# Weight parts and activations at the same offset modulo 256 bytes in a two-layer trunk

## The chip, the cores and the metric

The kernel runs on one core of a Trainium2 chip. The metric is the device time of one execution in microseconds (us); lower is better. TensorE (PE) multiplies, VectorE (DVE) and ScalarE (ACT) work elementwise, GpSimd (POOL) does a few small operations, and the DMA engines bring weights from HBM into SBUF, the on-chip memory of 128 partitions.

## What is computed

Two layers of a decoder trunk on 256 tokens of width 1024, in float32. A layer is a half-step FFN, four token mixers beside each other with gated merging, and a second half-step FFN. Almost all of the arithmetic is products of the activations with large weight matrices:

```
for l in range(DEPTH):
    h = _rmsnorm(x, ffn1_norm[l])
    x = x + 0.5 * _swiglu(h, ffn1_w_gate[l], ffn1_w_up[l], ffn1_w_down[l])   # 1024 -> 2816 -> 1024
    h = _rmsnorm(x, mix_norm[l])
    ... = jnp.split(h @ w_in[l], IN_SPLIT_POINTS, axis=-1)                    # 1024 -> 12288
    y_a, y_b, y_c, y_d = _hgrn2(...), _s5(...), _conformer_conv(...), _dilated_attention(...)
    merged = sum over k of gates[:, :, k] * (y_k @ w_branch[l, k])            # 512 -> 1024 each
    x = x + merged @ w_out[l]
    h = _rmsnorm(x, ffn2_norm[l])
    x = x + 0.5 * _swiglu(h, ffn2_w_gate[l], ffn2_w_up[l], ffn2_w_down[l])
return _rmsnorm(x, final_norm)
```

## The kernel before

**Three products for one.** TensorE reads operands of type float32r, of less precision than float32. So each operand is split in two: a high part, the value rounded to that type, and a low part, what is left. A product is then three matmuls into one PSUM bank (high by high, high by low, low by high):

```
def mm3(o, ah, al, bh, bl, first, last):
    T.matmul(o, ah, bh, start=first, stop=False)
    T.matmul(o, ah, bl, start=False, stop=False)
    T.matmul(o, al, bh, start=False, stop=last)
```

The first operand of `T.matmul` after the output is the stationary one (128 columns, loaded ahead of the matmul; the profile shows the load as PEld LDWEIGHTS), the second one streams through (the moving one).

**The weight stream.** `Stream` brings the weights through 512 slots of 1024 elements per partition, in the order in which they are used. A DMA on SyncE's queue lands 1 MB in one of four buffers `raw`; ScalarE writes the high part of a slot into one of six buffers `whi`, VectorE the low part into one of five buffers `wlo`:

```
self.act.activation(hv, src, AF.Copy)
self.dve.tensor_tensor(lv, src, hv.bitcast(F32), op=ALU.subtract)
```

Both run ahead of the matmuls by as many slots as there are buffers. Everything else (norms, evacuations, the mixers' small operations) is put between these by a planner that keeps an estimated clock for each engine; its order is fixed when the program is made.

**Two forms of product.** Activations are held feature-major, as parts `hTh` and `hTl` (after a norm), `gh` and `gl` (inside an FFN), `yAh` and so on (of the mixers).

- `cols_feat` and `rows_feat` make feature-major results: the weight part is stationary, the activations move, 256 columns. These are `gate_h` and `up_h` (FFN chunks 1 to 5), `pu_h`, `pf_h`, `pq_h`, `pb_h`, `pa_h`, `pgt_h` (mixer projections and gates), `glu` and `br`.
- `cols_tok` and `down` make token-major results: the activations are stationary, the weight part moves, 512 columns. These are `gate_t`, `up_t` (FFN chunk 0), `pi_t`, `pg_t`, `att_t`, `po_t` and `down`.

`down` sums over k = 0 to 21 (128 of the 2816 features each) into four banks, two token halves by two halves of the width. For k = 0 to 16 the four go together; for k = 17 to 21 first the one token half and then the other, and there k = 20 and 21 come last, first for the one half of the width and then for the other (6 matmuls each). The last FFN's second token half ends the program's matmuls.

**Where the tiles lie.** A pool gives each tag its buffers when the tag is first asked for, one after the other in a partition, with no alignment beyond 32 bytes. In bytes from the partition's start:

| tag | first buffer | step | start modulo 256 | holds |
|---|---|---|---|---|
| `ident`, `x0`, `x1` | 16512, 17024, 21120 | | 128 | identity, residual |
| `heap` | 25216 | 4096 | 128 | `hTh`, `hTl`, `gh0` to `gh4`, `gl0` to `gl4`, the mixers' parts, gates |
| `raw` | 119424 | 8192 | 128 | landed weights |
| `half` | 152256 | 2048 | 192 | `gh5`, `gl5` (the last chunk of 256), `sg`, `pT`, other temporaries |
| small constants | 172736 to 179391 | | various | `vcol` ... `amask`, `hmask`, `four`, `r4`, `mi`, `diag`, norm scalars |
| `whi` | 179392 | 4096 | 192 | high parts of the weights |
| `wlo` | 203968 | 4096 | 192 | low parts of the weights |
| small scratch | 224448 to 228511 | | various | `ropeA`, `ropeB`, softmax scalars, statistics |

The slices that a matmul takes of a tile begin at multiples of 512 bytes in it, so they keep the tile's offset modulo 256.

Of the kernel before, what the change touches and what calls it, by code (L numbers as in the profile page):

```python
# [19 lines left out]
P = 128  # L20
# [168 lines left out]
def trunk(ctx, tc, x_in, positions, ffn1_norm, ffn1_w_gate, ffn1_w_up, ffn1_w_down, mix_norm, w_in,  # L189
# [11 lines left out]
    def const(shape, name, dtype=F32):  # L201
        return sb.tile(shape, dtype, tag=name, name=name, bufs=1)
# [244 lines left out]
    amask = const([P, 3, 256], "amask")  # L447
    hmask = const([P, 4, 64], "hmask", mybir.dt.uint8)
    four = const([P, P], "four", I32)

    def range_reduce(dst, src, tag):
        k = H2(list(src.shape), "rr_k" + tag)
        V.tensor_scalar(k, src, 1.0 / TWO_PI, None, op0=ALU.mult)
        V.tensor_scalar(k, k, MAGIC, None, op0=ALU.add)
        V.tensor_scalar(k, k, MAGIC, None, op0=ALU.subtract)
        V.scalar_tensor_tensor(dst, k, -CW1, src, op0=ALU.mult, op1=ALU.add)
        V.scalar_tensor_tensor(dst, k, -CW2, dst, op0=ALU.mult, op1=ALU.add)
        V.scalar_tensor_tensor(dst, k, -CW3, dst, op0=ALU.mult, op1=ALU.add)
        V.tensor_scalar(dst, dst, math.pi, -math.pi, op0=ALU.min, op1=ALU.max)
# [1205 lines left out]
```

## Time and profile before

| | |
|---|---|
| three runs | 1583.33, 1577.35, 1583.43 us; median 1583.33 |
| the profiled execution | 1577.96 us, span 1576.3 us, mean granted TensorE clock 0.998 |
| busy in the span | PE 1550.6 us (98%), DVE 1106.4 (70%), ACT 839.6 (53%), POOL 28.1 (2%) |
| read from HBM | 277.53 MB, 178 GB/s over the span |

The span is the time from the first to the last instruction of one profiled execution; the device time beside it has 1.66 us more around it. The rows further down come from that execution. Nearly all instructions stand under L72, the line of the helper that issues them, so the names of the tiles tell them apart: `gate_h<-hTh,wlo` is a matmul into a bank of `gate_h` that reads `hTh` and `wlo`, without buffer numbers. A matmul's listed duration reaches from its start until its results are out, and overlaps with its neighbours'. The distance from one start to the next is what the stream of matmuls costs.

### The profile page before, as it was taken

To read this page: it belongs to the slowest core of one execution; us is meant where nothing else is said; L and a number is where in the kernel's file an instruction comes from. 1 tells how busy PE (TensorE), PEld (TensorE's weight loads), DVE (VectorE), ACT (ScalarE), POOL (GpSimd) and SP (SyncE) were. 2 spreads that over 40 slices of the span, in tenths; PEclk is the share of its full clock that TensorE was granted. 3 is DMA by queue.
4 is the path that set the end of the run, shared out by engine and by line. 5 is a ranking of instruction groups with operands and counts; after the bars stand their busy time and mean duration, and the time that the engine had idled before them with its cause. 6 is when DMAs were issued, how large, how long until landed. Compare 5 with 4: busy or idle time off the path is not lost.

```text
span 1576.3 us, 27619 instructions
## 1 busy us (share of the span) xinstructions
PE 1550.6 (98%) x11407; PEld 1417.4 (90%) x11407; DVE 1106.4 (70%) x1797; ACT 839.6 (53%) x1209; POOL 28.1 (2%) x58
## 2 busy tenths in 40 slices
PE   7999999999999999999999999999999999999998
PEld 5999789889899998999889988987899999989986
DVE  6778865976878866555478874568768897765553
ACT  5545555567565465444445543656665555554442
POOL 2000000000000000000000000000000000000000
PEclk9999999999999999999999999999999999999999
DMA  7565556553544556555565555665345445655551
GB/s 275 198 173 200 194 179 204 161 173 122 161 161 161 170 184 222 188 189 212 174 180 188 188 187 191 206 193 172 116 150 171 160 161 178 211 183 181 188 207 56
DMA packets 179518, 282.46 MB, mean 179 GB/s; under 512 B 26718, under 2 KB 82080, under 8 KB 179392
## 3 DMA queue, kind: packets, MB, share of 16 engines
q1 hardware_dynamic: 154240, 270.55, 51.4%
q10 hardware_dynamic: 24832, 9.97, 2.6%
q8 instruction: 89, 1.46, 0.4%
q14 instruction: 37, 0.30, 0.1%
q0 software_dynamic: 320, 0.18, 0.0%
HBM read 277.53 MB, written 3.15 MB: 178 GB/s over the span
## 4 chain that ended last, share of the span: by engine, by line
PE 91%; DVE 3%; ACT 2%; ACTq 1%; DMA 1%; issue 1%; POOL 0%; SPq 0%; POOLq 0%; DVEq 0%
PE down L72 15%; PE up_h L72 12%; PE gate_h L72 12%; PE att_t L72 11%; PE pgt_h L72 11%; PE br L72 6%; PE po_t L72 3%; PE gate_t L72 3%; PE up_t L72 2%; PE pi_t L72 1%; PE pb_h L72 1%; PE pu_h L72 1%; PE pf_h L72 1%; PE pa_h L72 1%; PE glu L72 1%; PE hl L72 1%
## 5 line engine op out<-in xcount | busy, mean ns | idle before, releaser
L72 DVE TENSOR_TENSOR wlo<-raw,whi 128x1024 fp32r<-128x1024 f32 x512 | 614.8, 1220 | 194.0 <-ACT whi L72 98.8
L72 ACT ACTIVATE whi<-raw 128x1024 fp32r<-128x1024 f32 x512 | 526.2, 1055 | 180.5 <-PE down L72 97.5
L72 PE MATMUL gate_h<-hTh,wlo 128*128 128x256 f32 x576 | 160.2, 278 | 2.8 <-DVE wlo L72 2.8
L72 PE MATMUL gate_h<-hTh,whi 128*128 128x256 f32 x576 | 161.1, 280 | 0.0
L72 PE MATMUL up_h<-hTh,whi 128*128 128x256 f32 x576 | 160.8, 279 | 0.2 <-ACT whi L72 0.2
L72 PE MATMUL up_h<-hTh,wlo 128*128 128x256 f32 x576 | 160.0, 278 | 0.8 <-DVE wlo L72 0.8
L72 PE MATMUL up_h<-hTl,whi 128*128 128x256 f32 x576 | 160.0, 278 | 0.0
L72 PE MATMUL gate_h<-hTl,whi 128*128 128x256 f32 x576 | 159.9, 278 | 0.0
L72 PE MATMUL pgt_h<-hTh,whi 128*128 128x256 f32 x512 | 145.6, 284 | 0.0
L72 PE MATMUL pgt_h<-hTl,whi 128*128 128x256 f32 x512 | 142.6, 279 | 0.0
L72 PE MATMUL pgt_h<-hTh,wlo 128*128 128x256 f32 x512 | 142.6, 279 | 0.0
L72 PE MATMUL down<-whi,gh 128*128 128x512 f32 x352 | 138.8, 394 | 0.0
L72 PE MATMUL down<-whi,gl 128*128 128x512 f32 x352 | 138.6, 394 | 0.0
L72 PE MATMUL down<-wlo,gh 128*128 128x512 f32 x352 | 138.2, 393 | 0.0
L72 PE MATMUL att_t<-whi,hTh 128*128 128x512 f32 x288 | 117.7, 409 | 0.0
L72 PE MATMUL att_t<-whi,hTl 128*128 128x512 f32 x288 | 113.5, 394 | 0.0
L72 PE MATMUL att_t<-wlo,hTh 128*128 128x512 f32 x288 | 113.0, 392 | 0.0
L72 PEld LDWEIGHTS gate_h<-hTh,wlo 128*128 128x128 f32 x576 | 108.2, 188 | 3.4 <-DVE wlo L72 3.4
L72 PEld LDWEIGHTS up_h<-hTh,whi 128*128 128x128 f32 x576 | 108.9, 189 | 0.6 <-ACT whi L72 0.4
L72 PEld LDWEIGHTS up_h<-hTh,wlo 128*128 128x128 f32 x576 | 108.1, 188 | 1.0 <-DVE wlo L72 1.0
L72 PEld LDWEIGHTS gate_h<-hTh,whi 128*128 128x128 f32 x576 | 108.8, 189 | 0.1
L72 PEld LDWEIGHTS gate_h<-hTl,whi 128*128 128x128 f32 x576 | 108.2, 188 | 0.0
(385 smaller groups left out, 3333.1 us busy)
## 6 DMA issues: line engine op xcount, KB each, us to landing
raw<-in_w_in_dram SPq DMA_DIRECT2D x60, 1024.0 KB, 5.1
raw<-in_ffn_w_up_dram SPq DMA_DIRECT2D x44, 1024.0 KB, 5.3
raw<-in_ffn_w_down_dram SPq DMA_DIRECT2D x44, 1024.0 KB, 4.9
raw<-in_ffn_w_gate_dram SPq DMA_DIRECT2D x42, 1024.0 KB, 5.1
raw<-in_w_in_dram SPq DMA_DIRECT2D x72, 512.0 KB, 4.7
raw<-in_w_branch_dram SPq DMA_DIRECT2D x16, 1024.0 KB, 5.1
raw<-in_w_out_dram SPq DMA_DIRECT2D x8, 1024.0 KB, 5.2
raw<-in_s_w_glu_dram SPq DMA_DIRECT2D x16, 256.0 KB, 3.8
```

The source lines that it names most:

```text
L72: return f(*args, **kw)
```

## The change

One tag is added to the pool, right behind `four`: a tile of 48 floats per partition, 192 bytes, that nothing writes or reads.

```
 amask = const([P, 3, 256], "amask")
 hmask = const([P, 4, 64], "hmask", mybir.dt.uint8)
 four = const([P, P], "four", I32)
+const([P, 48], "gap")
```

All tags that are first asked for after it begin 192 bytes further: `r4`, `mi`, `diag`, the norm's scalars, `whi` (179584, that is 128 modulo 256), `wlo` (204160, 128 modulo 256) and the small scratch at the end. `ident`, `x`, `heap`, `raw` and `half` stay where they are. No instruction is added, removed or moved.

## Rows read from the trace of the kernel before

**Rows 1.** Part 1 of the page: busy us, share of the span, instructions
```profile
PE 1550.6 (98%) x11407; PEld 1417.4 (90%) x11407; DVE 1106.4 (70%) x1797; ACT 839.6 (53%) x1209; POOL 28.1 (2%) x58
```

**Rows 2.** Waits of PE, longest first in total: us, times, longest us
```profile
PE xT L72 <- DVE xn L72: 9.1, 1, 9.1
PE hl L72 <- DVE KL L72: 3.3, 2, 1.7
PE gate_h L72 <- DVE wlo L72: 2.8, 2, 2.1
```

**Rows 3.** PE's groups, by form: count | busy us, mean ns of one | idle before
```profile
L72 PE MATMUL gate_h<-hTh,whi 128*128 128x256 f32 x576 | 161.1, 280 | 0.0
...
L72 PE MATMUL pgt_h<-hTh,whi 128*128 128x256 f32 x512 | 145.6, 284 | 0.0
...
L72 PE MATMUL down<-whi,gh 128*128 128x512 f32 x352 | 138.8, 394 | 0.0
...
L72 PE MATMUL att_t<-whi,hTh 128*128 128x512 f32 x288 | 117.7, 409 | 0.0
...
L72 PE MATMUL gate_t<-whi,hTh 128*128 128x512 f32 x64 | 26.7, 418 | 0.6 <-ACT hTh L72 0.6
...
L72 PE MATMUL pu_h<-hTh,whi 128*128 128x256 f32 x64 | 17.8, 279 | 0.0
...
L72 PE MATMUL pi_t<-whi,hTh 128*128 128x512 f32 x32 | 12.8, 400 | 0.0
```

**Rows 4.** The chain in order of time: start us, us, engine, line, count
```profile
222.21 11.31 PE pu_h L72 x96
...
287.05 19.25 PE att_t L72 x84
...
441.69 8.48 PE pgt_h L72 x72
478.55 9.90 PE pgt_h L72 x84
522.33 12.72 PE pgt_h L72 x108
...
572.72 10.88 PE br L72 x96
...
652.99 10.88 PE gate_h L72 x96
...
729.15 58.37 PE down L72 x255
...
1428.65 11.31 PE gate_h L72 x96
...
1507.80 53.20 PE down L72 x228
```

**Rows 5.** Busy us of each engine in two stretches, granted clock, DMA share, GB/s
```profile
652.99:718.27 65.28, 65.28 (x578) 65.28 (x578) 36.47 (x36) 30.16 (x36) 0.00 (x0) 1.00 0.60 197
1417.35:1496.50 79.15, 79.15 (x674) 79.15 (x674) 41.36 (x41) 35.18 (x42) 0.00 (x0) 1.00 0.56 186
```

**Rows 6.** Timeline of PE at the end: start us, us of one matmul
```profile
1562.18 0.39 PE L72 MATMUL down<-whi,gh 128*128 128x512 f32 x1
...
1566.30 0.39 PE L72 MATMUL down<-whi,gh 128*128 128x512 f32 x1
1568.80 0.39 PE L72 MATMUL down<-whi,gl 128*128 128x512 f32 x1
```

**Rows 7.** VectorE's and ScalarE's groups, by form, as in rows 3
```profile
L72 DVE TENSOR_TENSOR wlo<-raw,whi 128x1024 fp32r<-128x1024 f32 x512 | 614.8, 1220 | 194.0 <-ACT whi L72 98.8 <-PE down L72 64.8 <-PE gate_h L72 12.0
L72 ACT ACTIVATE whi<-raw 128x1024 fp32r<-128x1024 f32 x512 | 526.2, 1055 | 180.5 <-PE down L72 97.5 <-PE br L72 19.5 <-issue 13.5
...
L72 DVE TENSOR_TENSOR gl<-sg,gh 128x512 fp32r<-128x512 f32 x36 | 24.9, 693 | 25.1 <-ACT gh L72 25.1
...
L72 DVE TENSOR_TENSOR mrg<-mrg,gate 128x512 f32<-128x512 f32 x24 | 16.6, 692 | 0.8
```

More of the change, by code (lines that the diff above doesn't have):

```diff
@@ L449, in trunk @@
     four = const([P, P], "four", I32)
+    const([P, 48], "gap")
     def range_reduce(dst, src, tag):
```

## The prediction

> **What bounds the kernel now.** I read the page first for the share of the engines: TensorE is busy 98% of the 1576.3 us span, VectorE 70%, ScalarE 53% [rows 1]. The list of TensorE's own waits comes next, longest first: 9.1 us in one wait at the start, then 3.3 and 2.8 us [rows 2]. So the end is set by how fast TensorE goes from one matmul to the next; nobody keeps it waiting. The profiled run took 1577.96 us, 1.66 more than its span. The median of the runs is 1583.33, and two of the three lie there; the third, 1577.35, lies by the profiled one. I work from 1577.96 and come back to the gap of 5.4 below.
>
> **How fast the matmuls follow each other.** The busy time of a matmul overlaps its neighbour's, so the groups [rows 3] are of use for their counts only. The chain in order of time gives the pace: a piece "x96" is 96 matmuls one behind the other, and its time over its count is the distance from start to start. The reader is to see that one and the same work has two paces [rows 4]:
>
> - 256 moving columns (weights stationary, activations moving): `gate_h` at 652.99 takes 10.88/96 = 113.3 ns, `br` at 572.72 the same; `gate_h` at 1428.65 takes 11.31/96 = 117.8, and so do `pu_h` (11.31/96) and three pieces of `pgt_h` (8.48/72, 9.90/84, 12.72/108). A long stretch has the one pace or the other.
> - 512 moving columns (activations stationary, weights moving): `down` at 729.15 takes 58.37/255 = 228.9 ns, at 1507.80 it takes 53.20/228 = 233.3. `att_t` at 287.05 has 19.25/84 = 229.2.
>
> What differs is not the clock, nor the other engines. [...] What is left is TensorE's two reads from SBUF: each matmul streams its moving operand while the next stationary operand is loaded.
>
> **What the change touches.** By the layout above, every matmul with a weight part pairs a weight at 192 (modulo 256) with an activation at 128. One exception exists already: the last chunk of an FFN (`gh5`, `gl5`) lies in the `half` buffers, at 192, so the steps k = 20 and 21 of `down` have both operands at the same offset. They are the last 12 matmuls of the program, and the timeline has them [rows 6]: k = 17 to 19 of the second token half run from 1562.18 to 1566.30, 18 matmuls, 4.12/18 = 228.9 ns; then the first and the twelfth of k = 20 and 21 start at 1566.30 and 1568.80, 2.50/11 = 227.3 with times in hundredths, so between 226.4 and 228.2. Twice 113.3 is 226.7, which lies in that interval; I take 226.7 as the pace at equal offsets. The step happens within one accumulation, with nothing else altered, which is why I believe that the offset matters.
>
> **The sum, part by part.**
>
> - *512 columns.* Three groups per product: `down` 3 x 352, `att_t` 3 x 288, `gate_t`, `up_t`, `po_t` 9 x 64, `pi_t`, `pg_t` 6 x 32 [rows 3], 2688 in all. 96 of them are the exception (k = 20, 21, four FFNs, 24 each). Of the other 2592, 228 are at 233.3 and win 6.6 ns each: 1.5 us. 2364 at 228.9 win 2.2 each: 5.2. The 96 become unequal (192 against 128) and lose 2.2 each: 0.2. Together 6.5 us. Bounds: nothing, if the pace of the 12 has another cause, and, if 226.4 is the pace, 0.7 more.
> - *256 columns.* `gate_h` and `up_h` 6 x 576, `pgt_h` 3 x 512, ten products of 3 x 64 (`pu_h` is shown): 6912. No row has this form at equal offsets, so both ends are taken from its own two paces: all at 113.3, or all at 117.8. I take 113.3, since the equal-offset row of the nearest kind is twice that number. The gain is then what the slow stretches lose: the last FFN has 864 of them (nine pieces of 96, 11.31 - 10.88 = 0.43 each): 3.9 us; `pu_h`, `pf_h`, `pq_h` of the first layer 3 x 0.43 = 1.3; `pgt_h`, the three pieces shown, 264 x 4.5 ns = 1.2, and the same three again in the second layer, 2.4. Together 7.6 us; shorter slow pieces, of some dozens of matmuls, I leave out. The other end: 6912 x 4.5 ns = 31.1 more if all were slow, less the 7.6 that are lost already, a loss of 23.5 us.
> - *Everything else that is moved.* `r4`, `mi`, `diag` and the small scratch tiles go 192 bytes further and are no operands of those matmuls. VectorE's split (`wlo`, 1220 ns) and ScalarE's copy (`whi`, 1055 ns) now write at 128. VectorE's 512-element operations take 692 ns with every operand at 128 (`mrg`) and 693 with one at 192 (`gl`) [rows 7]: 1 ns, so nothing. For ScalarE no row tells offsets apart; it is idle more than half the time of those stretches, which hides it, and uncovered each 10 ns would cost 512 x 10 ns = 5 us. No instruction, wait or DMA is added: the gap is neither written nor read, and the landing zones `raw` stay where they are.
> - *What is late next.* TensorE 1% faster asks for weight parts 1% earlier. Their makers are busy 56 and 46% of such a stretch [rows 5], so I let nearly the whole gain through to the end.
>
> 7.6 + 6.5 = 14.1, and 1577.96 - 14.1 = 1563.9: **1564 us**. Against the median of 1583.33 that is 1.2%. The gap between the runs fits the same picture: one FFN going from the quick to the slow pace would cost 3.9 + 255 x 4.4 ns = 5.0 us, near the 5.4. If the pace no longer depends on chance, the runs after should also lie closer together than 6 us.
>
> [...]
>
> **The rivals.**
>
> 1. *No effect.* The pace of a stretch is settled by how it was entered, whatever the offsets, or another distance than that modulo 256 counts. For it: both paces occur at one and the same offset (256 columns). After the change the distance weights to activations is an odd multiple of 256, while for the 12 it is an even one. If the gap took no room, it would look the same. Against it: the step inside `down`. Time: as before, 1577 to 1584. Chance 0.10.
> 2. *Only the 512-column matmuls gain.* The 256-column ones go on falling into either pace. 1577.96 - 6.5 = 1571.5. Chance 0.08.
> 3. *The other side.* Equal offsets make the load and the moving stream of the 256-column matmuls meet all the time, and all feature-major stretches run at 117.8. Place: `gate_h`, `up_h`, `pgt_h`, the mixers' projections and `br`. For it: the equal-offset row exists only with the weights moving. Against it: load and stream are the same two reads there. Price: 23.5 - 6.5 = 17, so 1595. It decides when more than (7.6 + 6.5) us / 4.5 ns = 3,100 of the 6,912 are slow; now it is 864 + 288 + 528 = 1,680. Chance 0.11.
> 4. *A column every cycle.* [...] The twelve rows speak plainly against it: 0.01. [...]
>
> **How the numbers follow.** The forecast has 0.70, with its own range 1560 to 1569 (down by the 0.7 of the first bound and some 3 of the short pieces, up by some 5 for waits that open or a slow stretch that remains, one FFN being 3.9). The range, 1559 to 1580, takes in the forecast, rival 2 and the lower half of rival 1; it leaves out rival 3, rival 4, the upper half of rival 1 and a little of the forecast's tails, 0.2 together. This kernel's measurement can tell about 0.5% from no change, 8 us. Faster by more: the forecast and most of rival 2, 0.76. Within: rival 1, and rival 3 where it is only partly so, 0.15. Slower: the rest of rival 3, 0.09.
>
> **What would show it.** In the chain after, pieces of `gate_h`, `up_h`, `pgt_h` x96 at 10.88 everywhere, `down` at about 57.8 for 255, and `att_t` x84 at 19.04 in place of 19.25. In the last 12 matmuls, now unequal, 228.9 in place of 227. VectorE's and ScalarE's means unchanged, none of TensorE's waits after the start above 4 us. I am wrong if a 256-column stretch at 11.31 per 96 remains for a whole FFN, if `down` stays at 58.37, or if the paces fall as forecast and the span does not follow.

## The result, and the profile after

The change made the kernel slower: 1607.54 us, the median of four runs (1606.54 to 1608.89), against 1583.38 (1577.35 to 1583.66, four runs). The ratio is 1.0162, with a 95% interval from 1.0136 to 1.0188. The profiled execution took 1606.54 us, 28.6 more than the one of before, and its span is 1604.8 us. In the larger sets of runs further down the kernel before has medians of 1578.32, 1576.86 and 1574.45 us; measured against those the loss is 29 to 33 us and not 24.

First the shares of the engines, from part 1 of the page of the changed kernel, beside [rows 1]; then TensorE's longest waits, beside [rows 2].

```profile
PE 1579.7 (98%) x11407; PEld 1451.8 (90%) x11407; DVE 1107.9 (69%) x1797; ACT 838.9 (52%) x1209; POOL 27.7 (2%) x58
```

```profile
PE xT L72 <- DVE xn L72: 9.2, 1, 9.2
PE hl L72 <- DVE KL L72: 3.5, 2, 1.8
PE gate_h L72 <- DVE wlo L72: 2.1, 2, 1.4
```

The reader is to see that the same 11407 matmuls keep TensorE busy 29.1 us longer, while VectorE and ScalarE have what they had and no wait has grown by more than 0.7 us. So the loss lies in the distance from one matmul to the next. The makers of the weight parts, which now write at another offset, take the same time each (the groups of VectorE and of ScalarE, beside [rows 7]):

```profile
L72 DVE TENSOR_TENSOR wlo<-raw,whi 128x1024 fp32r<-128x1024 f32 x512 | 615.5, 1220 | 198.1 <-ACT whi L72 94.2 <-PE down L72 62.8 <-PE gate_h L72 13.8
```
```profile
L72 ACT ACTIVATE whi<-raw 128x1024 fp32r<-128x1024 f32 x512 | 525.7, 1054 | 179.7 <-PE down L72 95.2 <-issue 21.8 <-PE br L72 21.7
```

The chain in order of time (start, us, engine, count) has the answer to [rows 4]:

```profile
225.12 11.51 PE pu_h L72 x96
...
448.02 8.64 PE pgt_h L72 x72
...
583.52 11.52 PE br L72 x96
595.04 20.43 PE po_t L72 x90
630.54 10.88 PE up_t L72 x48
...
665.30 11.52 PE gate_h L72 x96
...
745.95 57.96 PE down L72 x255
...
1457.07 11.52 PE gate_h L72 x96
...
1537.71 51.76 PE down L72 x228
```

Every 256-column piece of 84 matmuls or more, in either layer and every product, has one pace: 11.52/96 = 120.0 ns (`pgt_h` 8.64/72 the same). Before there were two, 113.3 and 117.8; this is neither. The 512-column pieces became quicker: `down` 57.96/255 = 227.3 and 51.76/228 = 227.0, `up_t` 10.88/48 = 226.7, `po_t` 20.43/90 = 227.0.

The table by stretch, for about the 65 us that the first of [rows 5] covers:

```profile
653.78:719.00 65.22, 65.22 (x546) 65.22 (x545) 34.43 (x35) 29.46 (x36) 0.00 (x0) 1.00 0.56 186
```

The granted clock is 1.00, as in both stretches of [rows 5], and the same time holds 546 matmuls in place of 578. The ratio 578/546 is 1.059, and so is 120.0/113.3.

Last the end of the program, where k = 20 and 21 of `down` are now the unequal ones, 192 against 128 (timeline of TensorE; beside [rows 6]):

```profile
1590.69 0.39 PE L72 MATMUL down<-whi,gh 128*128 128x512 f32 x1
...
1592.54 0.39 PE L72 MATMUL down<-whi,gl 128*128 128x512 f32 x1
...
1594.80 0.40 PE L72 MATMUL down<-whi,gh 128*128 128x512 f32 x1
...
1597.37 0.39 PE L72 MATMUL down<-whi,gl 128*128 128x512 f32 x1
```

The last 12 start 2.57/11 = 233.6 ns apart, where 228.9 was forecast. Ahead of them, k = 17 to 19 have equal offsets: the first eight distances are 1.85/8 = 231, the next ten 2.26/10 = 226. A run needs some matmuls to settle.

### The profile page after: what moved, and what is told of

Same layout as the page of the kernel before. It is cut to its first block, busy times and chain, and to the rows that moved or that the text cites. A ratio compares the mean times of both kernels' runs of the same rounds, so it can differ in the third digit from the quotient of the medians.

```text
span 1604.8 us, 27619 instructions
## 1 busy us (share of the span) xinstructions
PE 1579.7 (98%) x11407; PEld 1451.8 (90%) x11407; DVE 1107.9 (69%) x1797; ACT 838.9 (52%) x1209; POOL 27.7 (2%) x58
## 4 chain that ended last, share of the span: by engine, by line
PE 91%; DVE 4%; issue 2%; ACTq 1%; ACT 1%; DMA 1%; SPq 0%; POOL 0%; POOLq 0%; DVEq 0%
PE down L72 15%; PE up_h L72 12%; PE gate_h L72 12%; PE pgt_h L72 11%; PE att_t L72 10%; PE br L72 6%; PE po_t L72 3%; PE gate_t L72 3%; PE up_t L72 2%; DVE wlo L72 2%; PE pb_h L72 1%; PE pq_h L72 1%; PE pf_h L72 1%; PE glu L72 1%; PE pu_h L72 1%
## 5 line engine op out<-in xcount | busy, mean ns | idle before, releaser
L72 DVE TENSOR_TENSOR wlo<-raw,whi 128x1024 fp32r<-128x1024 f32 x512 | 615.5, 1220 | 198.1 <-ACT whi L72 94.2
L72 ACT ACTIVATE whi<-raw 128x1024 fp32r<-128x1024 f32 x512 | 525.7, 1054 | 179.7 <-PE down L72 95.2
L72 PEld LDWEIGHTS up_h<-hTl,whi 128*128 128x128 f32 x576 | 110.6, 192 | 0.0
```

Of the source, the lines that this page charges most:

```text
L72: return f(*args, **kw)
```

## The experiments

In all of them the *distance* is the start of the stationary operand minus that of the moving one, modulo 256 bytes. Before, 256-column matmuls have +64 (weights stationary at 192, activations at 128) and 512-column ones -64; the change makes both 0. Every kernel here does the whole computation. Paces are start-to-start distances within one form, taken once at least five of a form have followed each other; of a piece of the chain, its time over its count.

The reading that the runs together will bear out: at distance 0 a matmul of 256 to 512 columns costs 0.417 ns a column, which is (226.7 - 120.0)/256, and 13.3 ns more: 106.7 + 13.3 = 120.0 for 256, 213.3 + 13.3 = 226.7 for 512. It is a reading from afterwards; no expectation below states it. These set other theories against each other: 256 columns leave the next load no time to spare; the role decides (stationary weights lose, moving weights win); distance does not matter, only where the weights lie; sizes and signs of the distance follow some simpler rule.

### Other distances, by the size of the gap

Three kernels differ from the changed one in one number, the gap's floats (the changed kernel has 48). Three more follow below.

```diff
-    const([P, 48], "gap")
+    const([P, 16], "gap")     e1_gap64: 64 bytes
+    const([P, 32], "gap")     e2_gap128: 128 bytes
+    const([P, 8], "gap")      e4_gap32: 32 bytes
```

> The gap is 64 bytes in place of 192, so the weight parts begin at 0 modulo 256 and lie 128 from the activations at 128, in both forms. Theory A (the pace hangs on the distance modulo 256 of the two operands, and 128 is the farthest that they can be apart): 256-column stretches at 113.3 ns and 512-column ones at 226.7, so about 1563 us, quicker than both kernels. Theory C (the distance counts modulo 128, so 128 is the same as 0): 120.0 and 226.9 as after the change, about 1607 us.

> The gap is 128 bytes: the weight parts begin at 64 modulo 256, 64 below the activations where before they lay 64 above. Theory A (distance with its sign, stationary minus moving): the 512-column matmuls get the distance +64 that the last twelve of the changed kernel have, 233.4 ns against 228.9, some 11 us more over 2592; for the 256-column ones, at -64, no row exists, 113.3 to 120. Theory D (the distance counts without its sign): everything as before, 113.3 and 117.8 mixed, 228.9, 1577 to 1584 us.

> The gap is 32 bytes: the weight parts lie 96 above the activations. Theory E (what counts is in which 64-byte line an operand begins): 96 above 128 is 224, the same line as 192, so the paces of before, 113.3 or 117.8 and 228.9, within 1577 to 1584 us. Theory A without lines: something between the paces at 64 and at 128.

Gap of 64 bytes (distance 128 for both forms): 1606.81 us (1606.32 to 1609.49) against 1578.32 (median of seven), ratio 1.0177, 1.0147 to 1.0207. Chain:

```profile
744.83 59.20 PE down L72 x255
...
1456.52 11.39 PE gate_h L72 x96
```

118.6 and 232.2 ns: the first form loses and the second too, so distance 128 is good for neither, against theory A, and 232.2 is not theory C's 226.9. That the time is the 1607 us of theory C is chance. Gap of 128 bytes (the two distances of before with exchanged signs, -64 and +64): 1600.97 us, ratio 1.0131, 1.0095 to 1.0166. Chain:

```profile
531.00 12.25 PE pgt_h L72 x108
...
742.97 59.47 PE down L72 x255
...
1453.03 11.31 PE gate_h L72 x96
```

`gate_h` is at 117.8 and `down` at 233.2. Of the 512 columns no long piece goes below 233 now. The 256 columns have both paces of before, but 113.3 (12.25/108) only in about a tenth of their steps, where before it was two thirds. So the sign counts, not only the size; theory D falls. Gap of 32 bytes (96 and 160): 1604.7 us in one run, 118.2 and 233.4, not the paces of before; theory E falls. Of the distances so far, with those of before and after, only +64 and -64 let 256 columns run at 113.3 for a whole piece, and only -64 and 0 let 512 go below 230.

### Is it the role or the columns?

The changed kernel with each 512-column matmul of `down` cut into two of 256. The offsets stay equal, the weights still move.

```diff
-                ns = slice(n * 512, (n + 1) * 512)
-                mm3(acc[t][n], gh[:, k % 4, tc_], gl[:, k % 4, tc_], hi[:, 0, ns], lo[:, 0, ns], k == 0, k == NK - 1)
+                for q in range(2):
+                    ns = slice(n * 512 + q * 256, n * 512 + q * 256 + 256)
+                    mm3(acc[t][n][:, q * 256:q * 256 + 256], gh[:, k % 4, tc_], gl[:, k % 4, tc_], hi[:, 0, ns],
+                        lo[:, 0, ns], k == 0 and q == 0, k == NK - 1 and q == 1)
```

> The changed kernel with each 512-column matmul of the down product cut in two of 256 columns, at equal offsets, weights still moving. Theory A (the number of columns decides: with 256 the next load has no time to spare): 120.0 ns each, so 240 in place of 226.9 for two, 2 x 960 matmuls, about 12.6 us more than the changed kernel, 1619 to 1621 us. Theory B (the role decides: equal offsets cost only where the weights are the stationary operand): 113.3 each, the same time as the changed kernel, about 1607 us.

1617.14 us in one run, 9.6 above the changed kernel's median. The chain:

```profile
749.11 61.13 PE down L72 x510
```

61.13/510 = 119.9 ns. Moving weights at 256 columns have the pace that stationary weights have, 120.0. The role (theory B) falls, the columns decide (theory A). The additive reading has the same 120.0 here; it parts from theory A's load without time to spare at sizes between 256 and 512, further down.

### Three more distances, and two offsets at once

```diff
-    const([P, 48], "gap")
+    const([P, 24], "gap")     e5_gap96: 96 bytes
+    const([P, 40], "gap")     e6_gap160: 160 bytes
+    const([P, 56], "gap")     e7_gap224: 224 bytes
```

> The gap is 96 bytes: the weight parts lie 160 above the activations (modulo 256). Theory L (only whole 64-byte steps of distance let two streams pass each other, and a step of 32 is like the worse neighbour): 118 to 120 ns per 256 columns, 232 to 234 per 512, 1600 to 1606 us. Theory M (the cost changes gradually with the distance): between the paces at 128 and 192, so 117.4 to 118.8, and for 512 columns between 229 and 232.6 the other way round.

> The gap is 160 bytes: the weight parts lie 32 below the activations. Theory L: 118 to 120 ns per 256 columns, 231 to 234 per 512. Theory M: between the paces at 192 and at 0, so 117.4 to 120.0, and 227 to 233.

> The gap is 224 bytes: the weight parts lie 32 above the activations. Theory L: 118 to 120 ns per 256 columns. Theory M: between the paces at 0 and at 64, so 114.7 to 120.0; for 512 columns (distance the other way) 227 to 229.

One run each, the kernel before at 1576.86 there (median of 16): 1619.86, 1596.54 and 1608.26 us. Their chains, in this order:

```profile
751.47 59.71 PE down L72 x255
...
1468.61 11.52 PE gate_h L72 x96
```
```profile
739.92 59.49 PE down L72 x255
...
1447.70 11.20 PE gate_h L72 x96
```
```profile
745.40 59.49 PE down L72 x255
...
1458.38 11.36 PE gate_h L72 x96
```

A gap of 96 bytes is the worst of all: 120.0 for 256 columns at distance 160, and 234.2 for 512 at 96. At 160 bytes `gate_h` has 116.7 (distance -32) and `down` 233.3 (+32); at 224 bytes, signs exchanged, 118.3 and 233.3. So 512 columns at 32 bytes either way from equality are as slow as far from it: nothing grades smoothly from 0 to 64, and theory M falls. -32 gives 256 columns 116.7, less than at 0 (120.0), less than most of -64 (117.8), and less than theory L's 118 to 120; +32 gives them 118.3. So no rule that goes by the size of the distance holds either.

The next kernel takes the good distance for each form. The buffers of `whi` and `wlo` get 1088 elements, and a slot is put at their start where the weights move (128, equal to the activations) and 16 floats on where they are stationary (192, distance +64 as before).

```diff
-NW, NRAW = 5, 4
+NW, NRAW, FEAT = 5, 4, 16
...
-        for loads, slots in groups:
+        for loads, slots, at in groups:
...
-        hi = self.pool.tile([P, 1024], FR, tag="whi", name=f"whi{self.n_high}", bufs=NW + 1)
+        hi = self.pool.tile([P, 1088], FR, tag="whi", name=f"whi{self.n_high}", bufs=NW + 1)[:, at:at + 1024]
...
-            lo = self.pool.tile([P, 1024], FR, tag="wlo", name=f"wlo{self.n_split}", bufs=NW)
+            lo = self.pool.tile([P, 1088], FR, tag="wlo", name=f"wlo{self.n_split}", bufs=NW)[:, at:at + 1024]
...
+                            FEAT if 256 * (i + 1) == w.shape[0] else 0))
```

The last line puts the two slots of k = 20 and 21 at 192, where `gh5` and `gl5` lie. To make room, `ropeA`, `ropeB` and `s5tt` go from the small scratch into `half`.

> Weight buffers of 256 bytes more, and each slot begins where its form wants it: at 128 for the 512-column matmuls (equal offsets, as after the change; at 192 where the activation part lies at 192), at 192 for the 256-column ones (64 above the activations, as before the change). The scratch of the rotary step and of the S5 tables moves into the half buffers to make room. Theory A (distance modulo 256, its sign and the number of columns decide): 226.9 per 512 columns, and for 256 columns the mix of 113.3 and 117.8 of before; 6.5 us less than the kernel before, or some 1571 us, with the same lottery of about 5 us between runs. If the buffers' pitch or the absolute address counted too, one of the two paces would differ from that.

1572.54 us, median of twelve runs (1567.85 to 1576.21), against 1576.86 of sixteen (1571.65 to 1582.98): ratio 0.9972, 0.9955 to 0.9989. This beats both kernels: by 0.3% the one before, which ran beside it, little but with an interval that excludes 1; and the changed kernel, which did not, by 35 us of medians. The chain:

```profile
222.17 11.31 PE pu_h L72 x96
...
729.88 57.88 PE down L72 x255
...
1427.11 10.88 PE gate_h L72 x96
...
1503.28 51.74 PE down L72 x228
```

`down` is at 227.0 as in the changed kernel, the 256 columns have their two paces back (`pu_h` 117.8, `gate_h` 113.3). The gain of 4.3 us lies below the prediction's 6.5 for the 512 columns, with an interval that holds it (1.7 to 7.1 us). The longer buffers also settle the modulus: 1088 elements are 4352 bytes, 17 times 256, so from one buffer to the next the distance changes by 256 bytes, and the paces stay as they were. One thing here is not explained: k = 20 and 21, at 192 and 192, come at 230 on average, not at 226.7. They are runs of 12 right after a change from 128 to 192, and may not have settled: in the first token half the last two of the twelve steps take 226. No kernel tried a longer run.

### Other columns at equal offsets

The changed kernel with `down`'s 512 columns cut unequally: 384 and 128 for the one half of the width, 320 and 192 for the other.

```diff
-                ns = slice(n * 512, (n + 1) * 512)
...
+                cut = (384, 320)[n]
+                for c0, c1 in ((0, cut), (cut, 512)):
+                    ns = slice(n * 512 + c0, n * 512 + c1)
...
```

> The changed kernel with the 512 columns of each down matmul cut into 384 and 128 in the one half of the width and 320 and 192 in the other, at equal offsets. Theory S (at equal offsets only a load that has no time to spare costs; behind more than 256 columns it has): 384 columns at 170.0 ns and 320 at 141.7, which is 113.3 per 256; 192 and 128 columns held up by their loads, 113 to 120 each. Theory P (256 columns are no threshold, each number of columns has its own pace, and 512 happens to be a good one): 384 and 320 each some 5 to 7 ns above that, about 176 and 148.

1652.84 us in one run. The sizes change every three matmuls, and the first of three takes some 200 ns for 384 and 320 columns, so a pace can hardly be read: 173 to 174 ns for the others of 384, 149 of 320, 111 of 192 and of 128 on average. A matmul of 320 costs more than in proportion to the columns (141.7), and that of 384 too (170.0). A second kernel therefore puts twelve of one size in a row:

```diff
-            down(0, k, slot)
-            down(1, k, slot)
+            down((0, 1), k, slot)
...
+            for c0, c1 in ((0, cut), (cut, 512)):
+                for t_ in t:
+                    tc_ = slice(t_ * P, (t_ + 1) * P)
+                    for n in halves:
...
```

with `cut` 384 in the first two FFNs and 320 in the last two.

> As the kernel with the cuts, but the pieces of one size stand in a row for both token halves and both halves of the width, twelve matmuls of 384 columns and then twelve of 128 (first, second FFN), twelve of 320 and then twelve of 192 (third, fourth), all at equal offsets, so that a pace can settle. Theory S (behind more than 256 columns a load has time to spare): settled, 170.0 ns for 384 columns and 141.7 for 320. Theory P (each number of columns has its own pace): 173 and 149 to 150 settled too, as in the runs of three.

1649.12 us in one run. Of the timeline, two runs of twelve; the first lines are the seventh matmul of 384 and the first of the 128 that follow, the last two the third and the twelfth of 320:

```profile
180.38 0.33 PE L72 MATMUL down<-whi,gh 128*128 128x384 f32 x1
...
181.42 0.22 PE L72 MATMUL down<-whi,gh 128*128 128x128 f32 x1
```
```profile
1002.42 0.31 PE L72 MATMUL down<-whi,gl 128*128 128x320 f32 x1
...
1003.74 0.31 PE L72 MATMUL down<-whi,gl 128*128 128x320 f32 x1
```

1.04/6 = 173.3 and 1.32/9 = 146.7 ns. Theory S, with 170.0 and 141.7, falls; theory P named 173 rightly and 149 to 150 not. At 0.417 ns a column the two are 160.0 + 13.3 and 133.3 + 13.3. With 256 and 512 there are four sizes on one line: 120.0, 146.7, 173.3, 226.7. The line ends below 256: matmuls of 192 and of 128 columns both come every 112 ns, where it would give 93.3 and 66.7; what holds them there is not shown.

### Equality, or the weights' own offset?

Two more kernels. One exchanges the offsets of the padded buffers: equal where weights are stationary, 192 where they move. The other has the distances of before at other addresses: a gap of 64 bytes ahead of every tile puts the activations at 192 and the weights at 0.

```diff
-NW, NRAW, FEAT = 5, 4, 16
+NW, NRAW, FEAT, TOK = 5, 4, 0, 16        e10_feat_equal; TOK goes where the moving weights had 0
...
```
```diff
+    const([P, 16], "gap")                ahead of all tags, e11_all_shifted
-    const([P, 48], "gap")
```

> The padded buffers again, with the two offsets exchanged: the 256-column matmuls have their weights at equal offsets with the activations, as after the change, the 512-column ones theirs 64 above, as before it. Theory A: 120.0 and 229.4, so the other half of the change alone: the time of the changed kernel and some 5.5 us, 1611 to 1615 us. If equal offsets alone were not the cause of 120.0, it would not show here.

> A gap of 64 bytes ahead of every other tile: activations at 192, weight parts at 0, the distances are those of before, 64. Theory A (only the distance counts): 113.3 and 117.8 per 256 columns, 229.4 per 512, 1572 to 1584 us. Theory F (the weights' own offset counts, and 0 is bad, as with the gap of 64 bytes behind the activations): 118.8 and 232.6, about 1606 us.

The kernel before had 1574.45 us there (median of 13). Equality for the 256 columns alone: 1612.47 us, ratio 1.0238, 1.0217 to 1.0260. Chain:

```profile
747.51 59.35 PE down L72 x255
...
1461.41 11.52 PE gate_h L72 x96
```

All of the loss is there (120.0), and `down` is back near its slower pace of before, 232.7. Everything shifted: 1574.17 us, ratio 0.9995, 0.9978 to 1.0013. Its chain:

```profile
652.89 11.31 PE gate_h L72 x96
...
889.68 10.88 PE gate_h L72 x96
925.68 58.36 PE down L72 x255
...
999.88 10.90 PE pu_h L72 x96
...
1430.67 10.88 PE gate_h L72 x96
```

With the distances of before come both paces (11.31/96 = 117.8 and 113.3) and the time of before, at other starts. The theory of the weights' own offset (F) falls; the distance is what counts, as far as one shift of everything can tell.

### The paces together

Mean ns from start to start over all such steps, all kernels of this study (two numbers: both occur, in long pieces). A piece shown above can differ from its mean by some tenths.

| distance | 256 columns | 512 columns |
|---|---|---|
| 0 | 120.0 | 226.7 |
| +32 | 118.3 | 233.3 |
| +64 | 113.3 or 117.8 | 233.3 |
| +96 | 118.2 | 234.3 |
| 128 | 118.8 | 232.6 |
| 160 (-96) | 120.0 | 233.4 |
| -64 | 117.8, in a tenth of the steps 113.3 | 228.9 or 233.3 |
| -32 | 116.8 | 233.3 |

A mean is not always a single step. At 0, and at +64 in a quick piece, each step is the same to 1 ns. The 228.9 of `down` before is a cycle of 229, 232 and 226; at 128 the steps of `gate_h` go 115, 118, 122, 120, 119.

## Why the prediction was wrong

**Right: what bounds the kernel, and that the offsets decide.** TensorE's distance from start to start is nearly all that moved. `whi` 1054, `wlo` 1220 ns are as before, and so nearly are the waits, so "everything else" was rightly nothing. The twelve rows of k = 20 and 21 meant what they were taken for.

**Right: the pace of the 512 columns; too large: their gain.** 226.7 at equal offsets came true, 227.3 and 227.0 with the starts of runs in it. The 96 exceptions lose some 5.5 ns each and not 2.2: they lie at +64 now (233.6), and the prediction gave them the 228.9 of -64. That alone makes 6.5 about 6.2. Added up from start to start over the profiled runs, the 512-column matmuls take 3.1 us less than before, and 5.1 less in the kernel with two offsets, whose median gained 4.3. In the changed kernel eight more of them than before came every 427 ns, at a granted clock of 0.50 (those of `att_t` from 336.80 to 340.10 us, for one, where before it was 1.00 in the same place); that is 1.6 us. The first matmuls of a run gained nothing.

**Wrong: the 256 columns.** The step that failed reads: "I take 113.3, since the equal-offset row of the nearest kind is twice that number." At 0.417 ns a column, 113.3 is 106.7 + 6.7 and 226.7 is 213.3 + 13.3. The step reads the 13.3 as a sixteenth of the 213.3. It is a constant: the cut `down` and the runs of 320 and 384 show 13.3 ns for all four sizes tried from 256 to 512. So equal offsets make 256 columns 120.0, and 226.7 being twice 113.3 is chance; the 113.3 belongs to distances of +64 and -64.

By the prediction's own sum, with 120.0 put in: 6912 x 6.7 = 46.3 us, less the 7.6 of pieces that were slow already, a loss of 38.7; less 6.2 gained; 1577.96 + 32.5 = 1610.5. Take off the 3 or so of the short slow pieces that the prediction left out (they too can lose only 2.2 ns), and some 1607 to 1608 comes out, where the profiled run has 1606.54. Part of that nearness is luck. Added up from start to start, the 256-column matmuls cost 34.2 us more than before (38.7 less 3 on paper), the 512-column ones 3.1 less (6.2 on paper), and the steps in which TensorE stood idle 2.6 less (nothing on paper); the rest is nearly nothing, and the sum is the 28.6 us between the two runs. So the 256 columns carry the whole loss, and no other cause is needed.

**The bounds.** Both ends for the 256 columns were paces that the form has at +64, so the truth lay outside them. One equal-offset row can be read as a sixteenth per column or as a constant per matmul; the second reading, 106.7 + 13.3, was the bound that was missing. So none of its three signs of being wrong named what came: a pace above 117.8.

**The rivals.** Rival 3 had the place and the sign: the feature-major stretches lose. That load and stream meet there is not shown. Its price was too low, 17 us for a pace of 117.8 where 120.0 came. Rival 1, that distance modulo 256 does not matter, is refuted by the chain: after the change the distance is an odd multiple of 256 and for the twelve rows it was an even one, and both have 226.7. Rival 2's other half, that the 256 columns go on falling into either pace, is refuted by it too.

**The spread.** Runs lie 2.35 us apart now, against 6.3, four runs each: as said, closer than 6. The kernel with the distances of before elsewhere has both paces, and 8.3 us between its ten runs. That with one pace left no lot is drawn fits this, but is not shown: only one run of each kernel has a chain.

**What stays open.** Which of two paces a stretch takes at +64 and -64, and how it enters it. Why equality costs 13.3 ns a matmul over its columns, and why the other distances cost what they do: the paces show that the distance between the starts of the stationary and the moving operand counts (226.7 to 234.3 ns for 512 columns, 113.3 to 120.0 for 256), not what in the hardware is behind it.

## What to carry to other kernels

Where matmuls with a load each follow one another without a wait, look at the start-to-start distance in the chain, form by form: two paces for one form under the same clock were a sign here that the operands' addresses matter, and the distance between the two operands' starts modulo 256 bytes is then worth a trial for each form by itself (here +64 for 256 columns, 0 for 512). A pace known for one size goes over to another only through a second size: two readings that agree on one row, so much per column and so much per matmul, differed here by 6.7 ns, 6912 times. And a bound taken from the values that a form has shown is no bound for a setting in which it has never run.

## What the runs showed that was not expected

- At equal offsets a matmul costs 13.3 ns over 0.417 ns a column: 120.0, 146.7, 173.3 and 226.7 ns for 256, 320, 384 and 512 columns. Any other distance that was tried costs 256 columns less or the same (113.3 to 120.0) and 512 columns more (228.9 to 234.3).
- Distances of 32 bytes to either side of equality have the 512 columns at 233.3 and the 256 at 118.3 and 116.8: the dependence is not smooth, and it has a sign.
- A new run can take time to settle: some eight matmuls after a change of offsets (231 ns and then 226, in the last lines of the profile after), about ten in the kernel with two offsets, and the first matmul after a change of the column count took some 200 ns at 320 and at 384 columns where the sizes change every three matmuls.
- Matmuls of 128 and of 192 columns come at the same 112 ns, at equal offsets in rows of twelve.
